# Fourier stage of a hybrid encoder block: who issues the gate loads, and where the output weights are split

## The chip, the cores and the metric

The kernel runs on one core of one Trainium2 chip. The metric is the device time of one execution in microseconds (us). TensorE appears as PE (its weight loads as PEld), VectorE as DVE, ScalarE as ACT, GpSimd as POOL, and SyncE as SP, which here only issues DMAs. A name such as SPq or ACTq is the DMA-issuing side of that engine.

## The reference

One encoder layer on x (2048 tokens, 1024 channels):

```python
hn = rms_norm(h, norm_w)
u_f, g_f, q, k, v, g_a = jnp.split(hn @ w_in, SPLIT_POINTS, axis=-1)
f = jnp.fft.fft2(u_f.reshape(B, S, 8, 64), axes=(1, 3), norm="ortho").real
y_f = jnp.einsum('bsgc,gcd->bsgd', f, w_fourier) * jax.nn.silu(g_f)
# q, k, v: three dilated window attentions, mixed by a softmax of their
# log denominators into o
y_a = o * jax.nn.silu(g_a)
return h + jnp.concatenate([y_f, y_a], axis=-1) @ w_out
```

The change touches what comes after the attention: the transform of u_f along the sequence, the gate g_f, and the output projection with w_out.

## The kernel before

Every matmul with large operands is made of three products of a high part and a low part of each operand (high times high, high times low, low times high), so a weight or an activation must be split before PE can use it: ACT writes the rounded high part, and DVE subtracts it for the low part.

Up to about 1167 us the kernel projects x and runs the attention. In that time the gates silu(g_f) are written to a DRAM buffer SG (4 blocks of 128 channels by 2048 tokens), and y_a, split in two halves yh, is stored to a DRAM buffer YA by SP (L743).

Then `tail_` runs the Fourier stage. The sequence transform is folded into four parts s = 0 to 3. `f_trans(s)` (L795 to L798) multiplies folded data F by a block matrix BD into four PSUM tiles ptr, which ACT and DVE split into `at` (L797, L798). `f_dft(s)` multiplies `at` with the split transform matrix `dt` for four blocks ct of 128 channels. For s = 0 and 2 ACT copies the sums to `pe` (L837). For s = 1 and 3 DVE forms sum and difference (L844, L845), and POOL multiplies them in place onto Y (L847, L848; the last two L847 of s = 3 run on DVE). Y holds the gates: `Y_dma` (L877 to L879) loads the four blocks of SG into it, 1 MB each, before.

`d_dma(s)` loads a raw transform matrix `dr`, `d_split(s)` splits it (L780, L781) and in between asks for the next. `wo_load` (L881 to L883) loads one raw block `wor` (128 by 512) of the output weights into one of three buffers, and `wo_prep(nh, ...)` (L885) is a generator: each step issues the load two blocks ahead and splits one block k (L894 and L895 for k < 4, L898 and L899 for k >= 4, with a scale). There are 8 steps for each half nh of the output columns: w0 and w1 in `tail_`.

Where these steps stand is written by hand: `f_trans` takes three steps of the generator that it is given after its own work, and `f_dft` takes some after each of its first three blocks:

```python
if ct < 3:
    for _ in range(3 if s else 2):   # s = 0 and s = 2
        next(fill, None)
...
if ct < 3:                           # s = 1 and s = 3
    next(fill, None)
    next(fill, None)
```

Each engine, and each engine's DMA issues, run in the order of the program. DMAs of SP and ACT take eight completion counters in turn (DMAHW0 to DMAHW7): before a DMA is issued, its engine waits until the DMA before it on the same counter has landed, whichever engine issued that one.

At the end `o_mm(r)` (L948, L951) runs the output projection, 48 matmuls of 512 columns for each block r of 128 tokens. Its first 24 need the y_a part of `mx`: `o_in0` loads YA transposed (L906), `o_mix_a(0)` makes high and low parts (L926 on ACT, L927 on DVE). The next 24 need the y_f part (`o_mix_y(0)`, L932 and L934).

Of the kernel before, what the change touches and what calls it, by code (L numbers as in the profile page):

```python
# [92 lines left out]
class Kernel:  # L93
# [716 lines left out]
    def f_dft(self, s, fill=iter(())):  # L810
        nc = self.nc
        V, A, G = nc.vector, nc.scalar, nc.gpsimd
        at, dt = self.AT.pop(s), self.DT.pop(s)
        par, sn = divmod(s, 2)
        if not sn:
            self.PE_ = self.fp.tile([128, 4, 512], F32, name="pe", tag="pe", bufs=1)
        for ct in range(4):
            cs = slice(ct * 128, ct * 128 + 128)
            q = sn and ct < 2
            ps = (self.psq, self.pss)[q].tile([128, 512], F32, name="pf", tag="qs"[q])  # L820
            jl = ((0, 0), (0, 1), (1, 0))
            if s < 2:
                for o in range(2):
                    mm = [(at[:, j, nt, cs], dt[:, l, nt, :256]) for nt in (2 * o, 2 * o + 1) for j, l in jl]
                    if s == o == 0:
                        mm += [(self.a5[:, j, cs], self.alr[:, :256]) for j in range(2)]
                    for i, (l, r) in enumerate(mm):
                        nc.tensor.matmul(ps[:, 256 * o:256 * o + 256], l, r, start=i == 0, stop=i == len(mm) - 1)  # L828
                ps = ps.rearrange("p (e k) -> p k e", e=2)
            else:  # L830
                mm = [(at[:, j, nt, cs], dt[:, l, nt]) for nt in range(4) for j, l in jl]
                for i, (l, r) in enumerate(mm):
                    nc.tensor.matmul(ps, l, r, start=i == 0, stop=i == len(mm) - 1)
            Y = self.Y[:, ct]
            sh = (lambda x: x.rearrange("p (k e) -> p k e", e=2)) if s < 2 else (lambda x: x)
            if not sn:
                A.copy(sh(self.PE_[:, ct]), ps)  # L837
                if ct < 3:
                    for _ in range(3 if s else 2):
                        next(fill, None)  # L840
                continue
            pe = self.PE_[:, ct]
            t1 = self.fp.tile([128, 512], F32, name="t1", tag="t1", bufs=3)
            V.tensor_tensor(sh(t1), sh(pe), ps, OP.add)  # L844
            V.tensor_tensor(sh(pe), sh(pe), ps, OP.subtract)  # L845
            lo, hi = Y[:, par:1024:2], Y[:, 2048 - par:1024:-2] if par else Y[:, 2046:1024:-2]
            (V if s == 3 and ct > 1 else G).tensor_tensor(lo, lo, t1, OP.mult)  # L847
            G.tensor_tensor(hi, hi, pe[:, 1 - par:], OP.mult)  # L848
            if s == 3 and ct == 0:
                self.o_in0()  # L850
            if s == 3 and ct == 2:
                self.o_mix_a(0)
            if ct < 3:
                next(fill, None)
                next(fill, None)
# [20 lines left out]

    def Y_dma(self):  # L877
        for ct in range(4):
            self.nc.sync.dma_start(self.Y[:, ct], self.SG[ct])  # L879

    def wo_load(self, nh, k):  # L881
        raw = self.WR[nh, k] = self.op.tile([128, 512], F32, name="wor", tag="wor", bufs=3)
# [364 lines left out]
    def tail_(self, pool, xp, fpool):  # L1247
        nc = self.nc
        for p in (self.gp, self.wp, self.wraw, xp):
            p.release()  # L1250
        yy, self.op = pool("yy"), pool("op")
        self.Y = yy.tile([128, 4, S], F32, name="Y")
        w = self.op.tile([128, 4, 2, 2, 512], F32R, name="wo0")
        wo = [[w[:, k // 2, :, k % 2] for k in range(KT)]]
        self.ap, self.dp2, self.fp = pool("ap"), pool("dp2", side="right"), pool("fp", side="right")
        w0 = self.wo_prep(0, wo[0])
        chn, cut = itertools.chain, itertools.islice
        self.d_dma(2)
        for k in range(2):
            self.wo_load(0, k)  # L1260
        self.Y_dma()
        flush = lambda g: [None for _ in g]
        s1, s2, s3 = self.d_split(1, 3), self.d_split(2), self.d_split(3)
        self.f_trans(0, s1)
        self.f_trans(1)
        ny = self.f_nyq()
        self.f_dft(0, chn(s2, cut(w0, 2)))
        self.f_trans(2)
        self.f_nyq_mul(ny)
        self.f_dft(1)  # L1270
        w = [fpool.tile([128, 2, 2, 512], F32R, name=f"wo1{i}", tag=f"F{i}") for i in range(3)]
        self.f_trans(3, cut(w0, 1))
        w.append(fpool.tile([128, 2, 2, 512], F32R, name="wo13", tag="F3"))
        wo.append([w[k // 2][:, :, k % 2] for k in range(KT)])
        w1 = self.wo_prep(1, wo[1])
        self.f_dft(2, chn(cut(w0, 3), s3, w0, w1))
        self.f_dft(3, w1)
        self.o_mix_y(0)
        for p in (self.fp, self.dp2):
            p.release()  # L1280
        self.yp = pool("yp", side="right")
        self.o_in(0)
        self.o_in(1)
        flush(w1)
        for r in range(NT):
            if r + 2 < NT:
                self.o_in(r + 2)
            self.o_mm(r, wo)
        for p in (self.yp, self.dp, fpool, self.ap, self.op, yy):
            p.release()  # L1290
# [21 lines left out]
```

## Time and profile before

| What | Value |
|---|---|
| median of 3 runs | 1410.32 us (1410.22 to 1411.82) |
| the profiled execution, own time | 1410.9 us |
| its span, first to last instruction | 1409.1 us, mean granted clock 0.998 |
| PE busy | 1381.4 us, 98% of the span |
| DVE, ACT, POOL busy | 992.7, 748.7, 459.7 us |
| Fourier stage on PE | about 1167 to 1222 us of the span |
| output projection on PE | from about 1222 us to the end |

The rows further down are read from the trace of the profiled execution. Times are counted from the start of the span. A bracket at the end of a row gives how long the engine was idle before the instruction, and what it is taken to have waited for. A weight load or a DMA issue runs beside the engine's other work.

### The profile page before, as it was taken

The page shows a single profiled execution, that of the slowest core. Times are in us where ns is not written, and L with a number is a line of the kernel's source. Part 1 is how long each engine was busy: PE and PEld are TensorE (multiplying, and loading weights), DVE is VectorE, ACT ScalarE, POOL GpSimd, SP SyncE. Part 2 cuts the span into 40 slices and gives each one's busy share as a digit, 9 for nine tenths or more (in the row PEclk, how much of TensorE's full clock was granted, in tenths as well). Part 3 has the DMA queues.
Part 4 walks back from the last instruction along what each step waited for, and adds up shares of the span by engine and source line. Part 5 has one row for each costly group of instructions (what it writes and reads, how often), then busy time and mean ns, then how long its engine had stood idle before and what let it go on. Part 6 is the DMA issues. An engine that isn't in the chain of part 4 may idle for free.

```text
span 1409.1 us, 27788 instructions
## 1 busy us (share of the span) xinstructions
PE 1381.4 (98%) x9506; PEld 1020.7 (72%) x9506; DVE 992.7 (70%) x3167; ACT 748.7 (53%) x2095; POOL 459.7 (33%) x639
## 2 busy tenths in 40 slices
PE   5999999999999999999999999999999999899998
PEld 3666666667777777778888888844448688788887
DVE  7888888878878888888887777744398887711111
ACT  6867767676757666666666565645213235410010
POOL 0255445444444444454433343320000101411110
PEclk9999999999999999999999999999999999999999
DMA  6876877786776767687766564545432526353432
GB/s 225 204 134 127 153 121 142 127 143 132 141 132 124 149 119 155 118 152 120 144 115 130 97 132 96 136 108 145 164 103 92 149 76 254 111 148 116 112 113 82
DMA packets 426829, 188.13 MB, mean 134 GB/s; under 512 B 320128, under 2 KB 410432, under 8 KB 426176
## 3 DMA queue, kind: packets, MB, share of 16 engines
q1 hardware_dynamic: 398084, 173.37, 56.3%
q10 hardware_dynamic: 28604, 13.00, 3.8%
q8 instruction: 74, 1.21, 0.4%
q14 instruction: 67, 0.55, 0.1%
HBM read 68.18 MB, written 29.76 MB: 70 GB/s over the span
## 4 chain that ended last, share of the span: by engine, by line
PE 82%; DVE 6%; issue 3%; DMA 3%; POOL 3%; ACT 2%; SPq 1%; POOLq 0%; DVEq 0%; ACTq 0%
PE psq L312 43%; PE py L948 13%; PE psq L574 12%; PE psq L590 5%; PE pS L461 3%; PE po L527 2%; PE po L528 1%; PE pS L449 1%; DVE xhl L223 1%; POOL ph L509 1%; DMA qw<-qw 1%; PE pf L828 1%; DMA wor<-in_w_out_dram 1%; POOL hl L376 1%; PE ptr L795 0%
## 5 line engine op out<-in xcount | busy, mean ns | idle before, releaser
L312 PE MATMUL psq<-wh,xT 128*128 128x384 f16 x4608 | 787.0, 327 | 3.3 <-ACT wh L289 1.5
L312 PEld LDWEIGHTS <-xT 128*128 128x128 f16 x4608 | 540.3, 119 | 193.8 <-issue 4.6
L497 ACT ACTIVATE P<-pS,ob,kb 128x256 f32<-128x256 f32 (+1 forms) x384 | 199.4, 527 | 150.5 <-DVE ob L489 150.1
L509 POOL TENSOR_TENSOR ph<-P,ph 128x512 f16<-128x512 f32 x160 | 189.5, 1184 | 196.4 <-ACT ph L504 184.1
L948 PE MATMUL py<-wo,mx 128*128 128x512 f32 x768 | 180.1, 397 | 3.8 <-DVE mx L927 3.8
L365 POOL TENSOR_TENSOR qn<-qn,kb 128x128 f32<-128x128 f32 x192 | 85.6, 446 | 293.7 <-DVE qn L364 201.9
L948 PEld LDWEIGHTS py<-wo,mx 128*128 128x128 f32 x768 | 146.1, 190 | 37.6 <-DVE mx L927 4.2
L574 PE MATMUL psq<-xT,wh 128*128 128x512 f16 x768 | 168.9, 379 | 0.0
L479 DVE CUSTOM_DVE_ANT_0 pS<-pS,bt 128x256 f32<-128x256 f32 (+1 forms) x384 | 147.7, 385 | 27.3 <-PE pS L449 18.8
L376 POOL TENSOR_TENSOR hl<-qn,hl 128x256 f16<-128x256 f32 x192 | 133.4, 695 | 29.7 <-ACT hl L371 29.7
L574 PEld LDWEIGHTS <-wh 128*128 128x128 f16 x768 | 74.1, 98 | 87.0 <-issue 0.8
L951 DVE TENSOR_TENSOR xo<-xo,py 128x512 f32<-128x512 f32 x32 | 22.0, 686 | 144.1 <-PE py L948 144.1
L538 DVE TENSOR_REDUCE ob<-po 128x128 f32<-128x256 f32 (+1 forms) x160 | 75.2, 470 | 54.1 <-PE po L528 54.1
L504 ACT CAST ph<-P 128x512 f16<-128x512 f32 x160 | 99.1, 619 | 9.4 <-DMA wr<-in_w_in_dram 1.6
L371 ACT CAST hl<-qn 128x256 f16<-128x256 f32 x192 | 77.1, 402 | 47.3 <-POOL qn L365 37.5
L332 DVE TENSOR_TENSOR vt<-psq,vt 128x128 f16<-128x128 f32 x192 | 55.0, 286 | 62.0 <-ACT vt L331 61.8
L331 ACT CAST vt<-psq 128x128 f16<-128x128 f32 x192 | 51.2, 267 | 82.8 <-PE po L528 82.8
L291 DVE SCALAR_TENSOR_TENSOR wh<-wr,nws,wh 128x384 f16<-128x384 f32 x128 | 86.5, 682 | 5.5 <-ACT wh L289 5.5
L590 PE MATMUL psq<-wh,xT 128*128 128x256 f16 x768 | 84.3, 273 | 0.0
L926 ACT CAST mx<-ya 128x512 fp32r<-128x512 f16 x16 | 9.9, 620 | 137.5 <-PE py L948 131.6
L590 PEld LDWEIGHTS <-xT 128*128 128x128 f16 x768 | 75.1, 98 | 9.1
L323 ACT COPY raw<-psq 128x256 f32<-128x256 f32 x192 | 69.4, 361 | 21.8 <-PE psq L312 21.4
(165 smaller groups left out, 1773.2 us busy)
## 6 DMA issues: line engine op xcount, KB each, us to landing
wr<-in_w_in_dram SPq DMA_DIRECT2D x104, 192.0 KB, 2.9
ot<-O SPq DMA_DIRECT2D x16, 792.0 KB, 4.5
st<-st SPq DMA_DIRECT2D x96, 128.0 KB, 2.4
xs<-in_x_dram SPq DMA_DIRECT2D x16, 512.0 KB, 6.9
xo<-in_x_dram SPq DMA_DIRECT2D x16, 512.0 KB, 3.6
out_dram<-xo SPq DMA_DIRECT2D x15, 512.0 KB, 3.0
O<-ob ACTq DMA_DIRECT2D x108, 66.0 KB, 2.5
O<-ob ACTq DMA_DIRECT2D x32, 132.0 KB, 2.7
```

The lines of the kernel that those rows point to most:

```text
L291: V.scalar_tensor_tensor(wh[:, 1, k - 1, :n], wr[k - 1], nws[:, k - 1:k], wh[:, 0, k - 1, :n], op0=OP.mult, op1=OP.subtract)
L312: nc.tensor.matmul(ps[:, :384], self.xtile(j, k, c, t), wh[:, l, k, :384], start=n == 0, stop=n == 23)
L365: G.tensor_tensor(qn[:, 2:4], qn[:, 2:4], self.kf[:, h0:h0 + 2], OP.mult)
L371: self.nc.scalar.copy(hl.rearrange("p a h l d -> p (a h) l d")[:, :, 0], qn)
L376: self.nc.gpsimd.tensor_tensor(hv[:, :, 1], qn, hv[:, :, 0], OP.subtract)
L479: V.tensor_tensor_reduce(out=sS[:, h, cs], in0=ps[:, h, cs], in1=bs, scale=1.0, scalar=-3.0e38, op0=OP.add, op1=OP.max, accum_out=mx[:, e, ...
L497: self.nc.scalar.activation(P[:, h, cs], sS[:, h, cs], AF.Exp, bias=ob[:, e, 130 + h:131 + h], scale=self.om[:, h0 + h:h0 + h + 1], accum_ ...
L504: self.nc.scalar.copy(ph[:, 0], P)
L509: self.nc.gpsimd.tensor_tensor(ph[:, 1], P, ph[:, 0], OP.subtract)
L574: nc.tensor.matmul(ps, wh[:, l, k, col * 128:col * 128 + 128], self.xT[:, j, k, ch * 512:ch * 512 + 512], start=n == 0, stop=n == 23)
L590: nc.tensor.matmul(ps[:, j * 256:j * 256 + 256], self.xT[:, i, k, r * 128:r * 128 + 128], wh[:, l, k, 128:384], start=n % 24 == 0, stop=n ...
L948: nc.tensor.matmul(ps[nh], m[:, j, k], wo[nh][k][:, l], start=(j, l, k) == (0, 0, 4), stop=(j, k) == (1, 3))
```

## The change

The four loads of the gates (L879) are issued by ACT instead of SP, and stand ahead of the first two loads of output weights in the program. The steps of `wo_prep` stand in other places: four of w0 instead of two in the first transform part, one after the third `f_trans` instead of none, three after the fourth instead of one, none instead of three in front of the last matrix split s3. `o_mix_a(0)` comes one block earlier in the last part.

```diff
--- before.py
+++ after.py
@@ -848,7 +848,7 @@
             G.tensor_tensor(hi, hi, pe[:, 1 - par:], OP.mult)
             if s == 3 and ct == 0:
                 self.o_in0()
-            if s == 3 and ct == 2:
+            if s == 3 and ct == 1:
                 self.o_mix_a(0)
             if ct < 3:
                 next(fill, None)
@@ -876,7 +876,7 @@
 
     def Y_dma(self):
         for ct in range(4):
-            self.nc.sync.dma_start(self.Y[:, ct], self.SG[ct])
+            self.nc.scalar.dma_start(self.Y[:, ct], self.SG[ct])
 
     def wo_load(self, nh, k):
         raw = self.WR[nh, k] = self.op.tile([128, 512], F32, name="wor", tag="wor", bufs=3)
@@ -1256,24 +1256,24 @@
         w0 = self.wo_prep(0, wo[0])
         chn, cut = itertools.chain, itertools.islice
         self.d_dma(2)
+        self.Y_dma()
         for k in range(2):
             self.wo_load(0, k)
-        self.Y_dma()
         flush = lambda g: [None for _ in g]
         s1, s2, s3 = self.d_split(1, 3), self.d_split(2), self.d_split(3)
         self.f_trans(0, s1)
         self.f_trans(1)
         ny = self.f_nyq()
-        self.f_dft(0, chn(s2, cut(w0, 2)))
-        self.f_trans(2)
+        self.f_dft(0, chn(s2, w0))
+        self.f_trans(2, cut(w0, 1))
         self.f_nyq_mul(ny)
         self.f_dft(1)
         w = [fpool.tile([128, 2, 2, 512], F32R, name=f"wo1{i}", tag=f"F{i}") for i in range(3)]
-        self.f_trans(3, cut(w0, 1))
+        self.f_trans(3, w0)
         w.append(fpool.tile([128, 2, 2, 512], F32R, name="wo13", tag="F3"))
         wo.append([w[k // 2][:, :, k % 2] for k in range(KT)])
         w1 = self.wo_prep(1, wo[1])
-        self.f_dft(2, chn(cut(w0, 3), s3, w0, w1))
+        self.f_dft(2, chn(s3, w0, w1))
         self.f_dft(3, w1)
         self.o_mix_y(0)
         for p in (self.fp, self.dp2):
```

ACT's order around the start of the Fourier stage, lines with + are new. YA<-yh is the store of a half of y_a, Y<-SG a gate load, and at<-ptr the first split of `f_trans(0)`; the names in brackets are the counters that are waited for:

```order
 L725 CAST yh<-yo 128x512 [waits DMAHW6_49,DMAHW7_49,DVE_49,Activation_49]
 L725 CAST yh<-yo 128x512 [waits DMAHW0_49,DMAHW1_49,DVE_49,Activation_49]
+L879 DMA Y<-SG 128x2048 x2
+L879 DMA Y<-SG 128x2048 [waits DMAHW2_49]
+L879 DMA Y<-SG 128x2048 [waits DMAHW5_49]
 L797 CAST at<-ptr 128x512 [waits PE_49] x4
 L804 CAST a_15470<-pm 1x512 [waits PE_49]
```

The four gate loads now stand between ACT's last cast of yh and its first cast of `at`; the third waits for counter 2 and the fourth for counter 5.

SP's order at the same place before the change (dr are raw transform matrices, wor raw output weights):

```order
L743 DMA YA<-yh 128x2x256 [waits DMAHW4_49,Activation_49]
L743 DMA YA<-yh 128x2x256 [waits DMAHW5_49,DVE_49]
L770 DMA dr<-in_dft_dram 128x2x512 [waits DMAHW6_49,Pool_49]
L770 DMA dr<-in_dft_dram 128x2x512 [waits DMAHW7_49]
L883 DMA wor<-in_w_out_dram 128x512 [waits DMAHW0_49]
L883 DMA wor<-in_w_out_dram 128x512 [waits DMAHW1_49]
L879 DMA Y<-SG 128x2048 [waits DMAHW2_49,PE_49]
L879 DMA Y<-SG 128x2048 [waits DMAHW3_49]
L879 DMA Y<-SG 128x2048 [waits DMAHW4_49]
L879 DMA Y<-SG 128x2048 [waits DMAHW5_49]
L770 DMA dr<-in_dft_dram 128x2x512 [waits DMAHW6_49,DVE_49]
```

And with the change:

```order
L743 DMA YA<-yh 128x2x256 [waits DMAHW5_49,Activation_49]
L743 DMA YA<-yh 128x2x256 [waits DMAHW6_49,DVE_49]
L770 DMA dr<-in_dft_dram 128x2x512 [waits DMAHW0_49,Pool_49]
L770 DMA dr<-in_dft_dram 128x2x512 [waits DMAHW1_49]
L883 DMA wor<-in_w_out_dram 128x512 [waits DMAHW3_49]
L883 DMA wor<-in_w_out_dram 128x512 [waits DMAHW4_49]
L770 DMA dr<-in_dft_dram 128x2x512 [waits DMAHW6_49,DVE_49]
L770 DMA dr<-in_dft_dram 128x2x512 [waits DMAHW7_49,DVE_49]
L883 DMA wor<-in_w_out_dram 128x512 [waits DMAHW0_49]
```

The gate loads are gone from SP. Where a row names a single counter it is the DMA's own, so counter 5 belongs, just before the fourth gate load, to the store of yh that waits for Activation here. The first load of wor waits for counter 3, which the first gate load has taken.

ACT's order in the third transform part (pe<-pf closes a block; wo_17290 is the first half of the weights, the other wo the second):

```order
 L837 COPY pe<-pf 128x512
 L780 CAST dt<-dr 128x1024 x2
-L898 ACTIVATE wo_17290<-wor,ysc 128x512
+L894 CAST wo_17592<-wor 128x512
 L837 COPY pe<-pf 128x512
-L898 ACTIVATE wo_17290<-wor,ysc 128x512
-L894 CAST wo_17580<-wor 128x512 x2
+L894 CAST wo_17592<-wor 128x512
+L894 CAST wo_17593<-wor 128x512 x2
 L837 COPY pe<-pf 128x512
-L894 CAST wo_17581<-wor 128x512 x2
```

The splits of the second half of the weights start ahead of the second block's copy, where the first half's were, and its first four are through before the third block's copy.

## Rows read from the trace of the kernel before

**Rows 1.** The page's busy times (busy us, share of the span, instructions by engine), and the table of waits for PE from 1170 to 1260 us of the span (waiting line, what it waited for: us in total, times, longest).

```profile
PE 1381.4 (98%) x9506; PEld 1020.7 (72%) x9506; DVE 992.7 (70%) x3167; ACT 748.7 (53%) x2095; POOL 459.7 (33%) x639
...
PE py L948 <- DVE mx L927: 3.8, 1, 3.8
PE ptr L795 <- DVE at L798: 0.2, 1, 0.2
```

**Rows 2.** The timeline of PE and DVE at the start of the output projection (start us, duration us, engine, line, operation, out<-in, shape, count, and in brackets the idle time before and what ended it).

```profile
1221.59 0.62 PE L948 MATMUL py<-wo,mx 128*128 128x512 f32 x2
1225.96 0.80 PE L948 MATMUL py<-wo,mx 128*128 128x512 f32 x1 [3.75 <-DVE mx L927]
...
1224.33 1.58 DVE L927 CAST mx<-ya 128x512 fp32r<-128x512 f16 x1
...
1239.50 0.69 DVE L951 TENSOR_TENSOR xo<-xo,py 128x512 f32<-128x512 f32 x1 [2.11 <-PE py L948]
...
1250.56 0.69 DVE L951 TENSOR_TENSOR xo<-xo,py 128x512 f32<-128x512 f32 x1 [4.78 <-PE py L948]
```

**Rows 3.** Stretches of the same place: window, its length, busy time of PE, PEld, DVE, ACT and POOL (instructions), granted TensorE clock (1.00 is 2.4 GHz, 0.50 is 1.2 GHz), DMA share, GB/s.

```profile
1222.00:1223.00 1.00, 0.21 (x1) 0.00 (x0) 1.00 (x2) 0.00 (x0) 0.00 (x0) 1.00 0.66 219
...
1224.00:1225.00 1.00, 0.00 (x0) 0.00 (x0) 1.00 (x2) 0.01 (x1) 1.00 (x1) 0.89 0.00 0
1225.00:1226.00 1.00, 0.04 (x1) 0.04 (x1) 1.00 (x2) 0.00 (x0) 0.62 (x1) 0.50 0.00 0
...
1230.00:1231.00 1.00, 1.00 (x4) 0.81 (x3) 0.92 (x1) 0.00 (x0) 0.37 (x1) 0.50 0.61 111
1231.00:1232.00 1.00, 1.00 (x5) 0.80 (x4) 0.00 (x0) 0.00 (x0) 0.00 (x0) 0.69 0.96 387
1232.00:1233.00 1.00, 1.00 (x6) 0.82 (x5) 0.00 (x0) 0.00 (x0) 0.00 (x0) 1.00 1.21 230
...
1240.00:1260.00 20.00, 20.00 (x88) 16.31 (x87) 2.92 (x6) 1.14 (x2) 1.29 (x1) 1.00 0.44 132
```

**Rows 4.** The timeline of PE, ACT and DVE at the start of the Fourier stage, columns as in rows 2.

```profile
1171.35 1.16 PE L795 MATMUL ptr<-BD,F 128*128 128x128 f32 x8
1172.71 2.94 PE L795 MATMUL ptr<-BD,F 128*128 128x128 f32 x24 [0.20 <-DVE at L798]
...
1170.12 0.62 ACT L725 CAST yh<-yo 128x512 f16<-128x512 f32 x1 [1.36 <-issue]
1170.64 2.04 ACT L797 CAST at<-ptr 128x512 fp32r<-128x512 f32 x4
...
1171.38 2.48 DVE L798 TENSOR_TENSOR at<-ptr,at 128x512 fp32r<-128x512 f32 x4
```

**Rows 5.** The SP queue at the same place (start us, us that the issues took, queue, line, tile, count), and the table of DMA issues (tile, queue, count, KB each, median us from issue to landing): the stores of YA from 1168 to 1172 us, those from 1095 to 1099 us that stood behind an O load, and the loads of Y.

```profile
1171.13 0.96 SPq L743 DMA_DIRECT2D YA<-yh  x2
...
1174.26 2.24 SPq L879 DMA_DIRECT2D Y<-SG  x4
...
YA<-yh SPq DMA_DIRECT2D x4, 128.0 KB, 2.0
...
YA<-yh SPq DMA_DIRECT2D x4, 128.0 KB, 5.5
...
Y<-SG SPq DMA_DIRECT2D x4, 1024.0 KB, 14.3
```

**Rows 6.** ACT's timeline around one of its own DMA issues late in the attention stage, columns as in rows 2.

```profile
984.59 0.37 ACTq L550 DMA_DIRECT2D O<-ob  x1
985.06 0.69 ACT L599 ACTIVATE scr<-psq,scb 128x512 f32<-128x512 f32 x1 [3.21 <-DVE ob L538]
```

**Rows 7.** ACT, DVE, POOL and the SP queue while the output weights are split, columns as in rows 2 and 5, with the table of DMA issues for the output weights (whole run) and for the transposes of YA (1140 to 1235 us).

```profile
1203.04 0.59 ACT L837 COPY pe<-pf 128x512 f32<-128x512 f32 x1 [2.55 <-POOL Y L848]
...
1205.75 2.00 ACT L780 CAST dt<-dr 128x1024 fp32r<-128x1024 f32 x2
...
1209.70 0.62 ACT L894 CAST wo<-wor 128x512 fp32r<-128x512 f32 x1
...
1217.41 0.73 ACT L898 ACTIVATE wo<-wor,ysc 128x512 fp32r<-128x512 f32 x1 [1.94 <-DMA wor<-in_w_out_dram]
...
1223.29 0.72 ACT L898 ACTIVATE wo<-wor,ysc 128x512 fp32r<-128x512 f32 x1 [1.67 <-DMA wor<-in_w_out_dram]
...
1204.80 1.42 DVE L899 SCALAR_TENSOR_TENSOR wo<-wor,ysc,wo 128x512 fp32r<-128x512 f32 x2
...
1219.40 3.08 DVE L899 SCALAR_TENSOR_TENSOR wo<-wor,ysc,wo 128x512 fp32r<-128x512 f32 x2
...
1220.13 1.81 POOL L848 TENSOR_TENSOR Y<-Y,pe 128x512 f32<-128x512 f32 x1
...
1211.58 2.54 SPq L906 DMA_TRANSPOSE ya<-YA  x2
1214.22 6.85 SPq L883 DMA_DIRECT2D wor<-in_w_out_dram  x4
...
wor<-in_w_out_dram SPq DMA_DIRECT2D x16, 256.0 KB, 3.4
...
ya<-YA SPq DMA_TRANSPOSE x6, 3.9
```

## The prediction

> **What bounds the kernel now.** I read the busy times first: PE works in 1381.4 us of a 1409.1 us span, and the table of its waits has only two entries in the stretch that the change touches, 3.8 us at L948 for L927 on DVE and 0.2 us at L795 for L798 [rows 1]. So a change here can move the end only by removing the first, by making the second longer, or by opening a new one. The timeline shows the first: PE issues two products of the output projection at 1221.59, the third needs the low part from L927, which DVE runs at 1224.33 for 1.58 us, and PE goes on at 1225.96 [rows 2].
>
> The wait costs more than its length. The granted clock falls during the 1225th us (0.89), is 0.50 from then on, and is full again only during the 1232nd (0.69) [rows 3]: PE stands still until 1225.96 and then works for over 5 us at 1.2 GHz. The sum is read off DVE's adds: the second add of block 1 starts 11.06 us after that of block 0 (1239.50 to 1250.56), which is 48 matmuls at full clock [rows 2, 3]. The first 48 began at 1221.59, so with no disturbance their add would have started at 1221.6 + 11.1 + 0.1 = 1232.8 instead of 1239.5. That is 6.7 us lost, 3.75 in the wait and 2.95 in the low clock.
>
> The second wait shows where PE is held at the start of the stage: it runs 8 products of `f_trans(1)` at 1171.35 and then waits for the second L798, which follows ACT's L797 that began at 1170.64; it goes on at 1172.71, so 2.07 us after ACT began [rows 4].
>
> **The change part by part.** *Gate loads on ACT.* They now stand between the last L725 (1170.12 to 1170.74) and L797 (1170.64) [rows 4]. An issue that waits holds what stands behind it on ACT: late in the attention stage L599 starts 0.47 us after the issue at 984.59, and its 3.21 us of idleness are put down to what that issue waited for [rows 6]. The first two gate loads wait for nothing new. The fourth waits for counter 5, which the first of the last two YA stores holds. SP issues that store at 1171.13 [rows 5], after ACT's L725, so nothing in the change makes it earlier. Its landing is the first unknown. The nearest row is its own: 2.0 us in this very place; the other end is 5.5 us, for the same stores behind an O load [rows 5]. Now some 3 MB of gates are under way on the same DMA engines when it goes out, so I take 2.6, close to its own row. The store lands at 1173.7, the issue takes 2.24/4 = 0.56 us [rows 5], and L797 starts at 1174.3 instead of 1170.64: 3.65 us late. PE's resumption moves with it, from 1172.71 to about 1176.4, since L798 and PE follow L797. Bounds: 2.0 and an issue of 0.47 give 3.0 us, 5.5 and 0.56 give 6.55 us. No gain is possible here, because the L797 that waits is the one that PE waits for.
>
> *The clock at that place.* PE would stand from about 1172.5 to 1176.4, 3.9 us. The only row of such a pause is the one in front of L948, 3.75 us, and there the clock fell 2.6 us after PE stopped at 1222.2 and came back 6.8 us later [rows 3]. With the same pattern it falls at 1175.1 and comes back at 1181.9, and the 5.5 us of work from 1176.4 on take twice as long as they need: 2.7 us lost. The other end is 0, if the pause just fails to bring the clock down. The nearest row is a pause of nearly this length that did, so I take 2.7. The Trainium skill (TensorE: Matmul & The Clock Gate, "HAM oscillation — how this bites in real kernels") says that a wait which idles PE sends it back to the throttled clock, and that each such wait pays for the warm-up again. By that rule the 2.7 us are paid, and the whole comes out slightly slower; without it the whole comes out slightly faster. The trace agrees at L948 (0.50 after 3.75 us) and has no second pause of this kind.
>
> *Loads on SP.* SP loses four issues, 2.24 us [rows 5], which nobody waited for. The first load of output weights now waits for the first gate load to land, because it takes the same counter. Y's loads took 14.3 us in one row with the matrix loads [rows 5]; alone in front, the first 1 MB should be done some 5 us after 1170.2, so SP goes on at about 1175.5 instead of 1173.2. The first weight is wanted by ACT no earlier than before, and all of ACT's work is 3.65 us later: cost 0, hidden by the shift itself; 0 to 2 us if a third or fourth weight arrives so late that ACT stands in front of the copies of `pe` and the splits of `f_trans(2)`.
>
> *Splits of w0 earlier.* Two pairs move into `f_dft(0)`, one to the third and two more to the fourth `f_trans`. PE has no wait between 1173 and 1221 [rows 1], and ACT and DVE have idle time there: ACT's L837 at 1203.04 had been idle for 2.55 us, waiting for POOL [rows 7]. Cost 0.
>
> *Splits of w1 earlier.* Before, ACT comes to w1 at 1209.70, after L837 at 1203.04, five splits, two copies and L780 (2.00 us), and ends it at 1223.29 [rows 7]. DVE's part there is slow where POOL works: two L899 take 1.42 us at 1204.80 but 3.08 us at 1219.40, beside L848 at 1220.13 [rows 7]. Now, counted as if the front had not moved, L837 (1203.0 to 1203.6, or half a us later since DVE has one more L899 ahead) and L780 (2.0) let w1 begin at about 1206.0. Three buffers rotate: load 3.4 us to landing, ACT 0.6 to 0.7, DVE 0.7, with the issue some 4.8 us for three [rows 7]. So block 3 is split on ACT at 1211, block 6 at 1216, block 7 at 1217. The two transposes of YA now follow all weight loads on SP instead of standing between them (at 1211.58 for 2.54 us [rows 7]): issued at about 1214.5 and 1215.8, landed 3.9 us later [rows 7], so 1219.7 at the latest.
>
> *L927.* DVE now has in order: L899 of block 6 (to 1217.3), L844 and L845 of the first transform block (1.4), L899 of block 7 beside POOL (1.5), L844 and L845 of the second (1.4), then L927: start at about 1221.7, end between 1222.1 and 1223.3 (0.4 alone, 1.58 beside POOL [rows 2]). PE wants it at about 1222.1, two products after 1221.6. The wait is 0 to 1.2, and I take 1.2, the row beside POOL. The y_f part follows with three DVE operations for each of two blocks, L932 and L934, and may hold PE for 0.4 us at its 25th product. Left over 1.6 us, too little to count on a fall of the clock; gain 6.7 - 1.6 = 5.1. Bounds: 6.7 if nothing is left, and about 2 if the splits keep their old pace of seven us for three and L927 stays late.
>
> **The sum.** Late start 3.65, clock there 2.7, gain at the projection 5.1: +1.25 us. The profiled execution took 1410.9 us by its own time, 0.6 above the median of 1410.32 and inside the three runs (1410.22 to 1411.82). I apply the sum to the median: 1411.5.
>
> **The rivals.** *The clock holds in front.* Then the sum is -1.45: 1408.9. For it: the trace has one such pause only, so nothing shows that each of them brings the clock down. Against: this one is no shorter.
>
> *The hold on ACT is short and the projection closes fully: faster.* 3.0 in front, no fall of the clock, 6.7 gained: 1406.6. If the issue hardly waits at all and costs only its 2.24 us from 1170.12 (L797 at 1172.4, 1.7 late) with 5.1 gained, 1406.9. For it: the store's own landing of 2.0. Against: the store is not issued before 1171.13, and every later instruction of ACT stands behind it.
>
> *The gates delay the store: slower.* The three gate loads that go out first take the DMA engines, and the store lands after 5.5 us instead of 2.6. Place: the fourth issue of L879; price 6.55 + 2.7 - 5.1 = +4.15, so 1414.5; it decides, against my forecast, from a landing of about 4.2 us on. For it: the row of 5.5 us behind an O load of less than 1 MB. Against: there the load stood in the same queue. The Trainium skill (DMA: Bandwidth & Descriptors, "Queues, rings and completion order") says that a DMA engine takes turns between the queues it has work for, so the store would share with the gates and not follow them; no row here shows two queues with megabytes each.
>
> *L927 stays late.* The splits keep the old pace, gain 2: 3.65 + 2.7 - 2 = +4.35, 1414.7.
>
> **How the numbers follow.** Forecast 0.36, clock holds 0.20, short hold 0.21, delayed store 0.17, L927 late 0.06. What a measurement here can tell from no change is 0.2%, 2.8 us, so 1407.5 to 1413.1. The forecast and the clock rival lie inside; a little of each spills over. Faster: 0.21 and 0.02; slower: 0.17, 0.06 and little more; the rest same. The range reaches into both outer cases, 1406.3 to 1414.9; the forecast's own, with a landing of 2.0 to 3.5 us and 0 to 2.5 us left at L948, is 1409.5 to 1413.3.
>
> **What would show it.** Right: ACT's L797 of `f_trans(0)` starts at 1173.5 to 1175.5 behind a gate load that waits for the YA store, PE's wait at L795 for L798 grows from 0.2 to 3 to 5 us, the clock is 0.50 for some us behind it, the wait at L948 is under 2 us and the clock full there. Wrong: L797 within 2 us of its old place (then faster), a wait at L948 of 3 us or more (then slower), or a new wait of PE between 1180 and 1220 for `at` or `pe`.

## The result, and the profile after

The changed kernel takes 1417.74 us (median of five runs, 1416.31 to 1418.38) against 1410.32 for the kernel before (1410.22 to 1412.18), measured together: a ratio of 1.005, with a 95% interval of 1.0038 to 1.0062. It is slower, by 7.4 us, and outside the forecast range. The profiled execution has a span of 1415.7 us where the one before had 1409.1.

The waits of PE from 1170 to 1260 us:

```profile
PE ptr L795 <- DVE at L798: 11.2, 1, 11.2
```

PE's timeline at the places of [rows 2, 4]:

```profile
1171.26 1.16 PE L795 MATMUL ptr<-BD,F 128*128 128x128 f32 x8
1183.59 5.21 PE L795 MATMUL ptr<-BD,F 128*128 128x128 f32 x24 [11.17 <-DVE at L798]
...
1212.27 22.64 PE L833 MATMUL pf<-dt,at 128*128 128x512 f32 x96
1234.75 55.54 PE L948 MATMUL py<-wo,mx 128*128 128x512 f32 x240
```

One wait is left where [rows 1] had two. The one at L795 has grown from 0.2 to 11.2 us, and the one at L948 is gone. PE goes on at 1183.59 instead of 1172.71, 10.88 us late, and its next 24 products take 5.21 us instead of 2.94. At L948 it is 13.16 us late (1234.75 against 1221.59), but at the end of the span only 6.6. So the projection gives back 6.6 us, about the whole of what it lost before.

ACT's timeline says who is late:

```profile
1170.03 0.62 ACT L725 CAST yh<-yo 128x512 f16<-128x512 f32 x1 [1.37 <-DVE yo L719]
1170.05 11.53 ACTq L879 DMA_DIRECT2D Y<-SG  x4
1181.62 2.05 ACT L797 CAST at<-ptr 128x512 fp32r<-128x512 f32 x4 [10.98 <-DMA YA<-yh]
```

The table of DMA issues from 1168 to 1172 us says what it waited for:

```profile
Y<-SG ACTq DMA_DIRECT2D x3, 1024.0 KB, 7.5
YA<-yh SPq DMA_DIRECT2D x4, 128.0 KB, 10.1
```

The four issues span 11.53 us, and L797 begins right behind them, 10.98 us later than in [rows 4]. Its idle time is put down to a store of YA, and these stores now land after 10.1 us (median of four), not after the 2.0 of [rows 5]. Stretches of the same time show the clock (columns as in [rows 3]):

```profile
1172.00:1174.00 2.00, 0.41 (x4) 0.22 (x2) 0.00 (x0) 0.00 (x0) 0.00 (x0) 1.00 0.96 389
1174.00:1176.00 2.00, 0.00 (x0) 0.00 (x0) 0.00 (x0) 0.00 (x0) 0.00 (x0) 0.68 1.01 412
...
1186.00:1188.00 2.00, 2.00 (x11) 2.00 (x11) 1.71 (x3) 0.87 (x2) 0.00 (x0) 0.50 0.92 279
1188.00:1190.00 2.00, 2.00 (x12) 0.94 (x10) 1.25 (x2) 0.59 (x1) 0.00 (x0) 0.91 1.04 390
...
1234.00:1236.00 2.00, 2.00 (x10) 1.60 (x10) 1.97 (x4) 0.00 (x0) 1.82 (x2) 1.00 0.00 0
```

While PE stands, the DMA engines are full (share about 1). The clock is at half until about 1188, and at 1234, where PE enters the projection, it stays full.

### The profile page after: what moved, and what is told of

Its sections match the earlier page's. It is cut to its first block, busy times and chain, and to the rows that moved or that the text cites. A ratio compares the mean times of both kernels' runs of the same rounds, so it can differ in the third digit from the quotient of the medians.

```text
span 1415.7 us, 27785 instructions
## 1 busy us (share of the span) xinstructions
PE 1381.6 (98%) x9506; PEld 1021.5 (72%) x9506; DVE 991.5 (70%) x3167; ACT 748.9 (53%) x2095; POOL 461.3 (33%) x639
## 4 chain that ended last, share of the span: by engine, by line
PE 80%; DVE 7%; issue 4%; DMA 3%; POOL 3%; ACT 2%; SPq 1%; ACTq 0%; POOLq 0%; DVEq 0%
PE psq L312 40%; PE py L948 13%; PE psq L574 12%; PE psq L590 5%; PE pS L461 3%; PE po L527 2%; PE pf L833 2%; POOL ph L509 1%; PE po L528 1%; DMA pt<-ph 1%; PE pS L449 1%; PE pf L828 1%; DVE xhl L223 1%; PE ptr L795 1%; POOL hl L376 1%
## 5 line engine op out<-in xcount | busy, mean ns | idle before, releaser
L948 PE MATMUL py<-wo,mx 128*128 128x512 f32 x768 | 177.3, 393 | 0.0
L948 PEld LDWEIGHTS py<-wo,mx 128*128 128x128 f32 x768 | 144.2, 188 | 32.9
L504 ACT CAST ph<-P 128x512 f16<-128x512 f32 x160 | 99.1, 619 | 11.2 <-DMA st<-st 2.4
```

The costliest lines, as they stand in the source:

```text
L504: self.nc.scalar.copy(ph[:, 0], P)
L948: nc.tensor.matmul(ps[nh], m[:, j, k], wo[nh][k][:, l], start=(j, l, k) == (0, 0, 4), stop=(j, k) == (1, 3))
```

## The experiments

Theory A: the loss is ACT standing at the fourth gate load, and the new places of the splits are a plain gain. The rivals stand in the expectations. Ratios are to runs of the kernel before on the same chip.

**The two halves of the change apart.** Only the splits, with the gate loads back on SP:

```diff
-            self.nc.scalar.dma_start(self.Y[:, ct], self.SG[ct])
+            self.nc.sync.dma_start(self.Y[:, ct], self.SG[ct])
...
-        self.Y_dma()
         for k in range(2):
             self.wo_load(0, k)
+        self.Y_dma()
```

> Only the new places of the splits; the gate loads are issued by SP again, behind the first two loads of output weights. Theory A (the loss is made by ACT, which stands at the fourth gate load until a YA store lands, and the new splits are a plain gain): L797 starts at about 1170.6 as in the kernel before, PE has no wait of 1 us or more behind 1173 and none at L948, the clock stays full at the projection: 1410.3 - 6.6 = 1403.7 us. Rival B (the new places of the splits are worth nothing by themselves, and the wait at L948 went only because the late front gave the splits 13 us more room): wait at L948 of 2 us or more, 1408 to 1411 us.

Only the gate loads, in the kernel before:

```diff
-            self.nc.sync.dma_start(self.Y[:, ct], self.SG[ct])
+            self.nc.scalar.dma_start(self.Y[:, ct], self.SG[ct])
...
+        self.Y_dma()
         for k in range(2):
             self.wo_load(0, k)
-        self.Y_dma()
```

> The kernel before with only the gate loads moved to ACT, ahead of the loads of output weights; splits as before. Theory A: L797 about 11 us late, PE's restart about 13 us late with the low clock, and the wait at L948 as before (3 to 4 us) with the clock drop behind it: 1410.3 + 13.2 = 1423.5 us. Rival B (the late front itself closes the wait at L948): no wait there, 1416 to 1418 us. Rival C (the splits' new places have a part in the long hold, by the loads of weights that they pull forward): L797 less than 6 us late, below 1418 us.

The gate loads alone took 1423.22 us (1.0095, 1.008 to 1.011), as theory A said. PE's waits show both costs side by side:

```profile
PE ptr L795 <- DVE at L798: 11.1, 1, 11.1
PE py L948 <- DVE mx L927: 3.7, 1, 3.7
```

So a late front does not close the wait at L948 by itself, and the splits have no part in the hold. Against the kernel before on its own chip this run loses 13.6 us and the whole change 7.4, so with the late front the new places are worth some 6.2 us.

The splits alone, however, took 1411.87 us (1.0013, 1.0004 to 1.0022), 8 us more than theory A said. It failed here. The waits of PE in that run, and below them ACT's timeline and the start of L833, in the kernel before and in that run:

```profile
PE pf L828 <- ACT pe L837: 2.8, 1, 2.8
PE ptr L795 <- DVE pe L845: 1.8, 1, 1.8
PE py L948 <- DVE mx L927: 1.2, 1, 1.2
```

```profile
1193.67 1.26 ACT L894 CAST wo<-wor 128x512 fp32r<-128x512 f32 x2 [9.95 <-DMA wor<-in_w_out_dram]
1194.84 0.58 ACT L837 COPY pe<-pf 128x512 f32<-128x512 f32 x1
```

```profile
1199.11 22.64 PE L833 MATMUL pf<-dt,at 128*128 128x512 f32 x96
...
1204.58 22.63 PE L833 MATMUL pf<-dt,at 128*128 128x512 f32 x96 [0.19 <-DVE pe L845]
```

The projection loses only 1.2 us, as it should. But the third and fourth pair, now in the first transform part, make ACT stand 9.95 us until their loads have come through behind 4 MB of gates. The last copy of `pe` stands behind them, and PE waits 2.8 us at L828 for that copy and then 1.8 us at L795 for L845 on DVE. PE comes to L833 at 1204.58 instead of 1199.11, 5.5 us late. Against 6.7 lost before, 5.5 + 1.2 leaves nothing.

**The same loads in another place.** `Y_dma()` on ACT, but behind `f_trans(1)`:

```diff
-        self.Y_dma()
         for k in range(2):
             self.wo_load(0, k)
...
         self.f_trans(1)
+        self.Y_dma()
```

> The changed kernel with the gate loads still on ACT, but written behind the second transpose stage, so that ACT's L797 of the first two stages stand ahead of them. Theory A (the place on ACT is what costs, not that ACT issues them): L797 starts at about 1170.6, the YA store has landed before the fourth load wants its counter, no wait of PE at L795 or L948: 1403 to 1405 us. Rival D (4 MB of gate traffic issued at once hurts wherever it stands, by holding up matrix and weight loads): a wait of PE of over 2 us at L828 to L833 or L948, 1406 us or more.

Three early on ACT, the fourth on SP:

```diff
-    def Y_dma(self):
-        for ct in range(4):
-            self.nc.scalar.dma_start(self.Y[:, ct], self.SG[ct])
+    def Y_dma(self, eng, cts):
+        for ct in cts:
+            eng.dma_start(self.Y[:, ct], self.SG[ct])
...
-        self.Y_dma()
+        self.Y_dma(self.nc.scalar, range(3))
         for k in range(2):
             self.wo_load(0, k)
+        self.Y_dma(self.nc.sync, range(3, 4))
```

> The changed kernel with three gate loads on ACT in the same early place, and the fourth on SP behind the first two loads of output weights. The 3 MB of early gates and the store beside them stay, the issue that waits for the store moves to SP. Theory A: the YA store still lands some 10 us after its issue, but L797 starts at 1171 to 1172.5 (three issues of 0.56 us): 1404 to 1406 us. Rival E (the early traffic itself delays the front, by PE's or ACT's own waits): L797 or PE's restart still 5 us or more late, 1410 us or more. If the store lands after 2 to 4 us here, the fourth load's own wait was not caused by the traffic.

The later place took 1410.31 us (1.0005, 0.9995 to 1.0014). L797 is not held, but PE waits 1.9 us at L828 for L837 and 1.3 us at L948: ACT stands 6.04 and 2.57 us for the third and fourth load of output weights. That is the cost of the early splits again, and in substance rival D, since these loads are late while the gates are under way. Three on ACT and one on SP took 1409.85 us (1.0001, 0.9991 to 1.001). This run separates the hold from the traffic. Its rows are ACT's and PE's timeline, and the table of DMA issues from 1168 to 1172 us:

```profile
1169.32 1.31 ACTq L879 DMA_DIRECT2D Y<-SG  x3
1170.67 2.05 ACT L797 CAST at<-ptr 128x512 fp32r<-128x512 f32 x4 [0.75 <-PE pm L802]
...
1172.63 2.94 PE L795 MATMUL ptr<-BD,F 128*128 128x128 f32 x24 [0.94 <-DVE at L798]
```

```profile
YA<-yh SPq DMA_DIRECT2D x4, 128.0 KB, 10.2
```

The stores land as late as in the changed kernel, after 10.2 us, and the hold of 11 us is gone. L797 begins right behind the three issues. The 0.75 us are put down to L802, but in the kernel before L797 did not wait for that: it began at 1170.64, and L802 ended at 1171.42. So the three issues themselves hold L797 for some 0.8 us, and PE's wait at L795 grows from 0.20 to 0.94 us. Theory A's first half holds: it is one issue with one wait, with ACT's work queued behind it. Both runs miss 1404 mostly by the price of the early splits. With three loads on ACT, PE waits 0.4 us at L828 for L837, 1.8 at L795 for L845 and 1.2 at L948.

**The dose.** The kernel of the last diff with one early load, and one with two (a single time each):

```diff
-        self.Y_dma(self.nc.scalar, range(3))
+        self.Y_dma(self.nc.scalar, range(1))
...
-        self.Y_dma(self.nc.sync, range(3, 4))
+        self.Y_dma(self.nc.sync, range(1, 4))
```

> The changed kernel with only the first gate load ahead on ACT, the other three on SP behind the first loads of weights. A dose of the traffic in front of the last two YA stores: 0 MB landed after 2.0 us (kernel before), 3 MB after 10.1. If a store lands when the bytes issued ahead of it are through (at 400 to 430 GB/s): 4.0 to 5.0 us. If the queues take turns and the store shares with the loads: 2 to 3 us. L797 within 1 us of 1170.6 in either case.

> The dose between: two gate loads (2 MB) ahead on ACT, two on SP behind the first loads of weights. The last YA stores took 2.0 us to land with 0 MB ahead of them, 5.5 with 1 MB, 10.1 with 3 MB. If the store waits for the bytes issued ahead of it: 7 to 8.5 us, about halfway. If it is a matter of the queue being used at all: 5 to 6 us as with one load. L797 within 1.5 us of 1170.6, since no issue on ACT waits.

The stores' landing from 1168 to 1172 us, with one load and then with two:

```profile
YA<-yh SPq DMA_DIRECT2D x4, 128.0 KB, 5.5
```

```profile
YA<-yh SPq DMA_DIRECT2D x4, 128.0 KB, 7.9
```

So 2.0, 5.5, 7.9 and 10.2 us for 0, 1, 2 and 3 MB: on the mean 2.7 us for each MB, or about 380 GB/s, close to what the DMA engines move in the stretches above (389 and 412 GB/s). One load delayed the stores by more than either theory allowed, two by as much as the first said. L797 began at 1169.76 and 1170.97, so ACT was not held. The times were 1409.57 and 1410.62 us.

**The price of the early splits.** Theory F: the third to fifth pair stand in the wrong place, and the gain is in the last part alone. All three kernels have the gate loads on SP as in the splits' run, and differ from it only here:

```diff
-        self.f_dft(0, chn(s2, w0))
-        self.f_trans(2, cut(w0, 1))
+        self.f_dft(0, chn(s2, cut(w0, 2)))
+        self.f_trans(2, w0)
```

> The new places of the splits with the gate loads on SP, but only two pairs of the first half of the weights stand in the first transform part (as before the change); three stand in the third transpose stage and three in the fourth, so that the last part is as in the changed kernel. Theory F (the new places cost by themselves what they gain: the third and fourth pair, put into the first transform part, make ACT stand at L894 until their loads have come through behind 4 MB of gates, near 1193, and the pe copy behind them holds PE): the 9.95 us hold of ACT stands behind all pe copies, no wait at L828 for L837; DVE's low parts may still stand in front of L844, 0 to 2 us; 1403 to 1407 us. Rival G (the splits gain nothing in the last part either): 1409 us or more with a wait at L948 of 2 us or more.

```diff
-        self.f_dft(0, chn(s2, w0))
-        self.f_trans(2, cut(w0, 1))
+        self.f_dft(0, chn(s2, cut(w0, 2)))
+        self.f_trans(2)
...
-        self.f_dft(1)
+        self.f_dft(1, cut(w0, 3))
```

> As the run before it, but the three pairs stand in the second transform part, between its blocks, where ACT has no work of the transform. Theory F: no wait at L828 for L837, none at L795 for L845 of over 0.5 us, wait at L948 of about 1.2 us as with the splits alone: 1403.5 to 1406 us, at least as good as the run before it. Rival G: 1409 us or more.

```diff
-        self.f_dft(0, chn(s2, w0))
-        self.f_trans(2, cut(w0, 1))
+        self.f_dft(0, chn(s2, cut(w0, 2)))
+        self.f_trans(2)
```

> As those, but between the first transform part and the fourth transpose stage nothing is split: two pairs in the first part as before, three in the fourth transpose stage instead of one, the other three behind those of the last matrix. Theory F with the gain coming from the places in the last part alone: no wait at L828 and L795, at L948 between 1.2 and 3 us, since two more pairs than in the runs before it are left for the last part: 1404 to 1408 us. If it needs the five pairs gone from the last part: wait at L948 over 3 us and 1409 us or more.

They took 1408.06 (0.9984, 0.9975 to 0.9994), 1406.12 (0.9973, 0.9964 to 0.9982) and 1407.73 us (0.9983, 0.9974 to 0.9993). All are faster than both kernels, and L828 waits for L837 in none, as theory F says. The first lies above the range of theory F, with a wait of 2.8 us at L795 for L845. With three pairs in the second transform part PE's waits are:

```profile
PE ptr L795 <- DVE pe L845: 1.7, 1, 1.7
PE ptr L795 <- DVE at L798: 0.2, 1, 0.2
PE pf L833 <- DVE pe L845: 0.2, 1, 0.2
```

Nothing is left at L948. The 1.7 us, more than I expected, come from DVE, where the low parts of these pairs stand between one block's L844 and L845 and the next block's, and ACT stands 4.12 us for the first of their loads. The traced execution was the longest of the ten (1408.67 us). In it the clock is near half from 1202 to 1206, and L833's 96 products take 24.18 instead of 22.64 us, so it does not show the median. In the third kernel nothing is lost before the projection. There PE waits only 0.2 us for L927, but 1.6 for L932 and 0.3 for L934, and the clock falls behind these.

**Three variants of the fastest.** Three weight loads ahead of the gates instead of two (the first step's load left out); the gate loads on ACT behind `f_trans(1)`; `o_mix_a(0)` back at its old block:

```diff
-        for k in range(2):
+        for k in range(3):
...
-            if n < 2 * KT:
+            if 2 < n < 2 * KT:
```

> The fastest so far (gate loads on SP, two pairs split in the first transform part, three between the blocks of the second) with three loads of weights instead of two put out ahead of the gate loads. If the rest of the cost is that the third load comes through behind the gates near 1194: its split is done by 1189, ACT's idle time in front of it goes, and PE's wait of 1.7 us at L795 for L845 shrinks below 1 us: 1404.5 to 1406 us. If the fourth load, which still stands behind the gates, holds DVE as long: the wait stays, 1405.5 to 1407 us.

```diff
-            self.nc.sync.dma_start(self.Y[:, ct], self.SG[ct])
+            self.nc.scalar.dma_start(self.Y[:, ct], self.SG[ct])
...
-        self.Y_dma()
...
         self.f_trans(1)
+        self.Y_dma()
```

> The fastest so far with the gate loads on ACT behind the second transpose stage instead of on SP. If who issues them is worth nothing once ACT doesn't wait: 1405 to 1407.5 us, L797 at about 1170.6. If freeing SP of them brings weights or matrices earlier: below 1405 us. If 4 MB on a second queue delay the first loads of weights and the matrix (their landing 5 to 6 us in that case): a new wait at L828, 1408 us or more.

```diff
-            if s == 3 and ct == 1:
+            if s == 3 and ct == 2:
```

> The fastest so far with the copies of the attention part (L926, L927) one block later in the last transform part, where they stood before the change. If that shift has a part in the gain at the projection: L927 starts some 3 us later (DVE's two operations of a block beside POOL and one more product) and PE waits 1.5 to 3 us at L948: 1408 to 1410 us. If L927 waits for the splits alone and not for its place: as the fastest, 1405.5 to 1407 us.

The first took 1406.17 us (0.9974, 0.9963 to 0.9984): the third load is early, ACT now stands 4.83 us for the fourth, and the wait for L845 stays, 1.8 us. The second took 1410.54 us (1.0007, 0.9998 to 1.0017): the loads issued later land later, and DVE stands 4.37 us in front of L875, which multiplies into Y, so that PE waits 4.6 us at L795 for L845. The third took 1409.24 us (0.9994, 0.9984 to 1.0003) with a new wait of 1.8 us at L948 for L927. The one-block shift is worth about 3 us here.

**Did the early splits cost the changed kernel anything?** The changed kernel as it is, gate loads early on ACT, with the pairs placed as in the fastest:

> The changed kernel as it is, gate loads early on ACT, with the three pairs between the blocks of the second transform part instead of the first part and the third transpose stage. If the late front already covers the wait for the third and fourth load (so that this cost is in the splits' run of 1411.9 but not in the changed kernel): the same time as the changed kernel, 1416 to 1419 us, with PE's wait of 11 us at L795 as its only one. If the early splits cost the changed kernel too: 2 to 5 us less, 1413 to 1415.5 us.

It took 1419.71 us (1.0068, 1.0051 to 1.0085), no faster than the changed kernel. PE waits 11.1 us at L795, and then 1.5 and 0.2 for L845, which is what the other place costs of its own; behind that L833 takes 24.17 us, as in the fastest kernel's trace. In the changed kernel ACT stood only 2.17 us for the fourth load:

```profile
1199.88 0.62 ACT L894 CAST wo<-wor 128x512 fp32r<-128x512 f32 x1 [2.17 <-DMA wor<-in_w_out_dram]
```

PE did not wait at all behind 1183.59: with a front 13 us late the loads have time to come through. So the early splits cost nothing there, and the miss is all in the front.

## Why the prediction was wrong

**The store's landing: the step that failed.** "Its landing is the first unknown ... so I take 2.6, close to its own row." It was 10.1, beyond my upper end of 5.5. The mechanism was named right: the fourth load waits for the store that holds counter 5, everything on ACT stands behind it, and PE with it. Put 10.1 for 2.6 into the sum and the late start is 1171.13 + 10.1 + 0.56 - 1170.64 = 11.15 us (measured 10.98), and the forecast 11.15 + 2.7 - 5.1 = +8.75, so 1419.1. The rival of the delayed store was this case with too small a price: its end was a row behind less than 1 MB, and I left it there although 3 MB were to stand in front. I also set that row aside because its load stood in the same queue; one gate load on the other queue gave the same 5.5 us. The rate of the DMA engines would have given the size.

I set the rival aside with the rule that the store would share with the gates. The traffic by queue (q10 carries ACT's gate loads, q1 what SP issues; packets, MB, share of 16 engines) shows what became of that. The rows are of 1172 to 1173, 1173 to 1174, 1176 to 1178 and 1180 to 1181 us:

```profile
q10 hardware_dynamic: 46, 0.38, 91.4%
...
q10 hardware_dynamic: 49, 0.40, 99.8%
...
q10 hardware_dynamic: 111, 0.78, 94.5%
q1 hardware_dynamic: 111, 0.06, 9.4%
...
q1 hardware_dynamic: 542, 0.33, 104.7%
q10 hardware_dynamic: 8, 0.01, 2.3%
```

From 1176 to 1178 both queues get 111 packets, but the gates' are of 7 KB and the stores' of 0.5 KB, so the stores get a thirteenth of the bytes. From 1172 to 1174, with stores issued from 1170.58 on, q1 has no packet at all, and 542 of its packets run only from 1180 to 1181, when the gates have 8 left. So the store lands when the big loads are through. The Trainium skill (DMA: Bandwidth & Descriptors, "Queues, rings and completion order") says that turns are taken packet by packet. The trace agrees from 1176 to 1178 us (111 and 111) and does not from 1172 to 1174 us (95 and none); read with the sizes, the rule spoke for the delay, not against it. Why the stores had no turn before 1174 stays open.

**The clock in front.** 2.7 us predicted; 24 products took 5.21 instead of 2.94 us, so 2.3. Right in size, in part by luck: the sum was built on a pause of 3.9 us, and the pause was 11.17 us. Whether the clock would have held through 3.9 us, as one rival has it, this result doesn't test.

**Loads on SP: cost 0.** No wait of PE shows a cost. SP's first two loads of output weights took 5.81 us to issue, where they took 0.94 before, and the late front hid it, as the prediction said it would, though the front was 13 us late and not 3.65.

**Splits of w0 earlier: "Cost 0."** True in the changed kernel, but for a reason that I did not give there. With the front on time they cost 5.5 us (the splits' run). Under the loads on SP I did name a third or fourth weight that comes late, at 0 to 2 us, but the cost of the new places was read from ACT's idle time at 1203, not from when the loads of the third and fourth block, behind 4 MB of gates, would be there. So the forecast had a second fault, which a hold of 11 us happened to hide: three early loads on ACT, without the hold, took 1409.85 us, where the sum with a cost of 0 gives some 1404.

**Splits of w1 and L927: gain 5.1, with 1.2 us of wait left.** Measured 6.6 in the changed kernel with no wait, and a wait of 1.23 in the splits' run, where the front is on time. The mechanism is right, and the size within its bounds (2 to 6.7); of the gain, the place of L927 one block earlier is worth some 3 us (measured in the fastest kernel). The rival in which L927 stays late is out.

**The sum.** 10.9 late start, 2.3 clock, -6.6 at the projection (what is left of the spans' difference): +6.6. Against the forecast the front is 6.8 us worse and the projection 1.5 better.

## What to carry to other kernels

Before a DMA issue goes onto an engine that computes, look up what its completion counter waits for, and price that transfer with all the bytes that will be in flight beside it, on other queues too. Move a wait to a queue with nothing urgent behind it: the same loads, three on ACT and one on SP, cost no hold. A split moved forward is free only if its load is there at that time; two edits that hide each other's cost must be run apart.

## What was not expected of the hardware

A small store waited for large loads on another queue: 128 KB took 10.2 us to land beside 3 MB of loads, 2.0 without. Whether a store of larger packets would fare better was not tried.

The length of a pause did not tell whether the clock falls. After 2.81 us without work at L828, in the splits' run, it stayed full; after 1.87 us at the same place, in the run with the gate loads behind `f_trans(1)`, it fell between 1194 and 1195, when PE had gone on at 1192.84, and 24 products took 4.35 us instead of 3.07. The two pauses and the stretches behind them, columns as in [rows 2, 3], first the splits' run:

```profile
1195.48 3.10 PE L828 MATMUL pf<-dt,at 128*128 128x256 f32 x24 [2.81 <-ACT pe L837]
...
1196.00:1197.00 1.00, 1.00 (x11) 1.00 (x10) 1.00 (x2) 1.00 (x3) 0.00 (x0) 1.00 0.75 215
1197.00:1198.00 1.00, 1.00 (x11) 1.00 (x10) 1.00 (x3) 1.00 (x2) 0.00 (x0) 1.00 0.75 283
```

```profile
1192.84 4.35 PE L828 MATMUL pf<-dt,at 128*128 128x256 f32 x24 [1.87 <-ACT pe L837]
...
1194.00:1195.00 1.00, 1.00 (x8) 1.00 (x7) 1.00 (x3) 1.00 (x3) 0.00 (x0) 0.62 0.73 236
1195.00:1196.00 1.00, 1.00 (x7) 1.00 (x6) 1.00 (x3) 0.36 (x1) 0.00 (x0) 0.50 0.07 27
```

The runs with one and with two early loads show it at the same length: PE paused 1.83 us at the same place in both, and behind it L833 ran at the low clock for a while in the first (granted clock 0.50 from 1203 to 1205) and at full clock in the second (1.00 from 1202 to 1210):

```profile
1201.33 1.13 PE L795 MATMUL ptr<-BD,F 128*128 128x128 f32 x8 [1.83 <-DVE pe L845]
1202.65 24.14 PE L833 MATMUL pf<-dt,at 128*128 128x512 f32 x96 [0.19 <-DVE pe L845]
```

```profile
1202.44 1.13 PE L795 MATMUL ptr<-BD,F 128*128 128x128 f32 x8 [1.83 <-DVE pe L845]
1203.75 22.62 PE L833 MATMUL pf<-dt,at 128*128 128x512 f32 x96 [0.19 <-DVE pe L845]
```

The difference, 1.5 us, is as large as some of the gains above, which is why they rest on medians and not on one trace. What tells the pauses apart was not tried, and stays open.
